# An RWKV scan in a two-layer network: substitution of two chunks at once, four product buffers, preparation in halves

## The chip, the core and the metric

The kernel is one program on one core of a Trainium2 chip. The metric is device time in microseconds from one launch to its end. Five engines work beside each other, each in the order of its own queue, and wait for one another by semaphores: TensorE (PE; its weight loads PEld), VectorE (DVE), ScalarE (ACT), GpSimd (POOL) and SyncE (SP), which issues the DMAs.

## The reference, cut to what matters

The network takes 256 context rows and 256 latent rows of 1,024 columns, in float32. Its first layer mixes them with RWKV-7 and Mamba side by side; attention, experts and a second block of two layers follow. The change lies in the RWKV part: per head (8 heads of 64 x 64) a state runs over 256 context rows and then over 256 latent rows, once forward and once backward.

```python
def step(S, inp):                       # per row: r, w, k, v, a, b
    sa = jnp.einsum('bhvk,bhk->bhv', S, a_t)
    S = S * w_t[:, :, None, :] + sa[..., None] * b_t[:, :, None, :] + v_t[..., None] * k_t[:, :, None, :]
    return S, jnp.einsum('bhvk,bhk->bhv', S, r_t)
...
logw = rw_w0 + tanh(lw) @ rw_w_up;  decay = exp(-exp(-softplus(-logw) - 0.5))
iclr = sigmoid(rw_a0 + la @ rw_a_up)
kk = k * rw_k_k / max(norm(k * rw_k_k), 1e-12)          # norm per head
k_dir = k * (1 + (iclr - 1) * rw_k_a);  a = -kk;  b = kk * iclr
bonus = (sum(r * k_dir_f * r_k0) + sum(r * k_dir_b * r_k1)) * v
```

## The kernel before, in words

Channels lie on partitions and rows on columns. `mixer_in` leaves the projections in `zrw` (12 blocks of 128 channels x 512 rows: k, r, v) and `lg` (low-rank inputs). The RWKV stage then runs in three parts.

*Preparation* (`rwkv_prep`, L646): for all 512 rows, in four blocks `j` of 128 channels and both directions `d`, low-rank products (L675, L682) with full 128-row weights, sigmoids, a running sum `cs` of the decay within each chunk (L679), `kd` (L685, L686), the scaled k (L689) and `b` (L691, on GpSimd). The three arrays `cs`, `b`, `kd` have their own memory, on the other side of the working space.

*Scan* (`rwkv`, L693): both directions at once, in eight steps of 64 rows. Forward takes the chunks 0 to 7, backward 3, 2, 1, 0, 7, 6, 5, 4. For step `n`:
- `products(n)`: scaled factors `ar` and `bkp` (L734 to L741, on DVE and GpSimd), their products on TensorE (L750), masked into `g` by DVE (L751), and the transposed `bkp` into `bt` (L758, L760). `bkp` has one buffer, `ar`, `g` and `bt` three.
- `base(n)`: inverts the 16 x 16 diagonal blocks of (1 - lower part of `g`) by forward substitution on DVE: cuts (L768 to L771), then 15 steps of a shuffle (L777), a product (L780) and a sum (L782), 8 heads x 16 columns wide and narrower at each step.
- `inverse(n)`: expands them into `st` (L788) and doubles the blocks twice, each time with a DVE transpose (L793), a mask on GpSimd (L796), products on TensorE (L800, L804), ACT in between and a sum (L805).
- `values(n)`: v transposed by products with the identity (L815), evicted by ACT.
- `through(n)`: the recurrence. State X times `ar` (L829) plus `g` times v (L832), evicted as `z`, times `st` (`up_`, L836), evicted, the state's update on TensorE (L843) and DVE (L848, L849), and the output (L854 to L861).

In program order the loop takes `through(n)`, `values(n+1)`, `inverse(n+1)`, `base(n+2)`, `products(n+3)`, then the bonus and `rwkv_out` of a half where it is complete, then `FILL` = 6 chunks of modulation (`ada_rest`, L396 to L405: 256 KB weight loads and products, 26 chunks in all, independent of the scan).

*Handover*: `layer0` halves the results into `cathi` and `catlo` (L947, L948) and starts the output projection (`mix_out`), whose weights come by SP (L329) and are split by ACT and DVE (L347, L348).

The order on each engine isn't written out by hand here: `TileContext(nc, schedule_with_timeline_sim=True)` lets a planner choose it with its own costs, in which an earlier place in the program gives precedence. A tile's buffer is given out again when its last reader is done.

Of the kernel before, what the change touches and what calls it, by code (L numbers as in the profile page):

```python
# [26 lines left out]
FILL = 6  # L27
# [66 lines left out]
def host_arrays(inp):  # L94
# [75 lines left out]
    lo = _Pack()  # L170
    for d in range(2):
        lo.add(f"w_up{d}", _rows_to(g["rw_w_up"][0, d], at=32 * d))
        lo.add(f"a_up{d}", _rows_to(g["rw_a_up"][0, d], at=64 + 32 * d))
    lo.add("g_up", _rows_to(g["rw_g_up"][0]))
    A["lora"] = lo.array()
# [14 lines left out]
    return A, pk.at, lo.at, {name: pack.at for name, pack in cst.items()}  # L190
# [75 lines left out]
class Net:  # L266
    def __init__(self, ctx, tc, ins, at, out):
        self.tc, self.nc, self.ins, self.out = tc, tc.nc, ins, out
        self.par_at, self.lora_at, self.cst_at = at
# [376 lines left out]
    def rwkv_prep(self, zrw, lg, arr, pool):  # L646
        nc = self.nc
        mm = nc.tensor.matmul
        lora = pool.tile([P, 2048], F32, name="lora", bufs=1)
        nc.sync.dma_start(lora, self.ins["lora"][:, :2048])  # L650
        o = {n: a for n, (a, _) in self.lora_at.items()}
        reset = pool.tile([P, T], F32, name="reset", bufs=1)
        nc.gpsimd.memset(reset, 1.0)
        nc.gpsimd.memset(reset[:, ::64], 0.0)
        tl = pool.tile([P, T], F32, name="tl", bufs=1)
# [5 lines left out]
        nc.sync.dma_start(lg[:, 0], self.ins["lora"][:, 2048:2560])  # L661
        ssp = self.bank(2, [8, T])
        for j in range(4):
            kq = pool.tile([P, T], F32, name="pq")
            nc.scalar.activation(kq, zrw[:, j], AF.Square, scale=self.p("k_k", j))
            mm(ssp, self.c("sel")[:, 8 * j:8 * j + 8], kq, start=j == 0, stop=j == 3)
        nrm = pool.tile([8, T], F32, name="pq")
        nc.scalar.activation(nrm, ssp, AF.Sqrt)
        nc.vector.tensor_scalar(nrm, nrm, 1e-12, None, op0=ALU.max)
        nc.vector.reciprocal(nrm, nrm)  # L670
        for j in range(4):
            ic = [pool.tile([P, T], F32, name=f"ic{d}") for d in range(2)]
            for d in range(2):
                wp = self.bank(0, [P, T])
                mm(wp, lora[:, o[f"w_up{d}"] + j * P:o[f"w_up{d}"] + (j + 1) * P], tl, start=True, stop=True)  # L675
                sg = pool.tile([P, T], F32, name="pq")
                nc.scalar.activation(sg, wp, AF.Sigmoid, bias=self.p(f"w0{d}", j))
# [3 lines left out]
                ap = self.bank(1, [P, T])  # L681
                mm(ap, lora[:, o[f"a_up{d}"] + j * P:o[f"a_up{d}"] + (j + 1) * P], tl, start=True, stop=True)  # L682
                nc.scalar.activation(ic[d], ap, AF.Sigmoid, bias=self.p(f"a0{d}", j))
                kd = arr["kd"][:, d, j]
                nc.vector.tensor_scalar(kd, ic[d], self.p("k_a", j), ka1[:, j:j + 1], op0=ALU.mult, op1=ALU.add)  # L685
                nc.vector.tensor_mul(kd, kd, zrw[:, j])  # L686
            rp = self.bank(3, [P, T])
            mm(rp, self.c("selt")[0:8, j * P:(j + 1) * P], nrm, start=True, stop=True)
            nc.vector.scalar_tensor_tensor(zrw[:, j], zrw[:, j], self.p("k_k", j), rp, op0=ALU.mult, op1=ALU.mult)  # L689
            for d in range(2):  # L690
                nc.gpsimd.tensor_mul(arr["b"][:, d, j], zrw[:, j], ic[d])  # L691

    def rwkv(self, zrw, arr, lg, y, pool, fill):  # L693
# [7 lines left out]
        first, second = (up, dn), (dn, up)  # L701
        bcast = lambda m, n: m[:, None, :].to_broadcast([m.shape[0], n, m.shape[1]])
# [10 lines left out]
        S16 = {}  # L713

# [6 lines left out]
        def products(n):  # L721
            ch, tok = tokens(n)

# [4 lines left out]
            ar = AR[n] = pool.tile([P, 2, 4, P], F32, name="ar", bufs=3)  # L728
            for d in range(2):
                a0, b0 = first[d], second[d]  # L730
                cs = arr["cs"][:, d, :, tok[d]]
# [6 lines left out]
                nc.vector.tensor_mul(bkp[up, d, :, 0, a0], arr["b"][up, d, :, tok[d]], ei[up, d])  # L738
                nc.gpsimd.tensor_mul(bkp[dn, d, :, 1, a0], arr["b"][dn, d, :, tok[d]], ei[dn, d])
                nc.gpsimd.tensor_mul(bkp[up, d, :, 0, b0], arr["kd"][up, d, :, tok[d]], ei[up, d])  # L740
                nc.gpsimd.tensor_mul(bkp[dn, d, :, 1, b0], arr["kd"][dn, d, :, tok[d]], ei[dn, d])  # L741
# [3 lines left out]
            g = G[n] = [pool.tile([P, 8, P], F32, name=f"g{d}", bufs=3) for d in range(2)]  # L745
            for d in range(2):
                for odd, r in ((0, up), (1, dn)):
# [5 lines left out]
            bt = BT[n] = pool.tile([P, 2, 4, P], F32, name="bt", bufs=3)  # L753
            tp = [self.bank(1, [P, 2, 4, 64]) for _ in range(2)]
            for d in range(2):
                for j in range(4):
                    for odd, r in ((0, up), (1, dn)):
                        tr(tp[odd][:, d, j], bkp[r, d, j, odd], ident[r, r])  # L758
            for odd, r in ((0, up), (1, dn)):
                ev(bt[:, :, :, r], tp[odd])  # L760

        def base(n):

            c32 = pool.tile([P, 8, 32], F32, name="c32", bufs=1)
            for q in range(4):
                rq = slice(32 * q, 32 * q + 32)
                at = 64 * (q // 2) + 32 * (q % 2)
                nc.vector.tensor_copy(c32[rq], G[n][q // 2][rq, :, at:at + 32])  # L768
            c16 = pool.tile([P, 8, 16], F32, name="c16", bufs=1)
            nc.vector.tensor_scalar(c16, c32[:, :, 0:16], self.c("half")[:, 0:1], None, op0=ALU.mult)  # L770
            nc.vector.scalar_tensor_tensor(c16, c32[:, :, 16:32], self.c("half")[:, 1:2], c16,  # L771
                                           op0=ALU.mult, op1=ALU.add)
            s = S16[n] = pool.tile([P, 8, 16], F32, name="s16")
            nc.gpsimd.tensor_copy(s, bcast(self.c("id16"), 8))
            for k in range(15):
                lb = pool.tile([P, 8, 16], F32, name="lb", bufs=3)
                nc.vector.stream_shuffle(lb[:, :, k + 1:], c16[:, :, k + 1:],  # L777
                                         [16 * (q // 16) + k for q in range(32)])
                m = pool.tile([P, 8, 16], F32, name="lm", bufs=2)
                nc.vector.tensor_mul(m[:, :, k + 1:], lb[:, :, k + 1:],  # L780
                                     s[:, :, k:k + 1].to_broadcast([P, 8, 15 - k]))
                nc.vector.tensor_add(s[:, :, k + 1:], s[:, :, k + 1:], m[:, :, k + 1:])  # L782

        def inverse(n):
# [3 lines left out]
            nc.vector.tensor_mul(st.rearrange("p h (g c) -> p h g c", g=4),  # L788
# [18 lines left out]
        def values(n):  # L807
# [3 lines left out]
            vr = pool.tile([P, 4, 64], F32, name="vr", bufs=1)  # L811
            nc.gpsimd.tensor_copy(vr, zrw[:, 8:12, tok[1]])
            for d, rows in ((1, up), (0, dn)):
                for j in range(4):
                    mm(vp[rows, j], vr[:, j] if d else zrw[:, 8 + j, tok[0]], ident, start=True, stop=True,  # L815
                       skip_group_check=True)
                ev(uv[rows, d], vp[rows].rearrange("p j (h v) -> p (j h) v", h=2))

        def through(n):
# [19 lines left out]
            if n < 7:  # L839
                for d in range(2):  # L840
# [23 lines left out]
        products(0)  # L864
        base(0)
        values(0)
        inverse(0)
        products(1)
        base(1)
        products(2)  # L870
        for n in range(8):
# [4 lines left out]
            if n < 6:  # L876
                base(n + 2)
            if n < 5:
                products(n + 3)
            if n in (3, 5):  # L880
                self.bonus(n // 4, zrw, arr)
# [10 lines left out]
    def bonus(self, half, zrw, arr):  # L892
# [3 lines left out]
        for j in range(4):  # L896
            e = arr["b"][:, 1, j, at]
            nc.vector.tensor_scalar(e, arr["kd"][:, 0, j, at], self.p("r_k0", j), None, op0=ALU.mult)
            nc.vector.scalar_tensor_tensor(e, arr["kd"][:, 1, j, at], self.p("r_k1", j), e,
# [50 lines left out]
    def layer0(self, run, late):  # L950
# [3 lines left out]
        with ExitStack() as mix:  # L954
# [15 lines left out]
            with ExitStack() as ph:  # L970
                self.stream(ph, RAWS, 512, 0, "right")
                arrp = pool(ph, "arr", side="right")
                arr = {k: arrp.tile([P, 2, 4, T], F32, name=k) for k in ("cs", "b", "kd")}
                with ExitStack() as c:
                    self.rwkv_prep(zrw, lg, arr, pool(c, "pw", 2))
                with ExitStack() as c:
                    rw = pool(c, "rw", 2)
                    self.rwkv(zrw, arr, lg, cat[:, 0:4], rw, self.ada_rest([(0, n) for n in range(8, 24)] + [(1, n) for n in range(EARLY)], rw, 0, 1))
# [1068 lines left out]
```

## Time and profile before

| | |
|---|---|
| median of 3 runs | 3051.7 us (3050.88 to 3053.53) |
| profiled execution | 3049.1 us, span 3047.3 us |
| TensorE busy | 2935.5 us, 96% of the span |
| DVE busy | 2113.2 us, 69% |
| ACT busy | 1592.5 us, 52% |
| GpSimd busy | 774.2 us, 25% |

Busy shares are means over stages with different limits; the stage of the change (some 230 to 570 us) is read by itself. A group of instructions gives its line, engine, operation, tiles out<-in, shapes and count, then the busy time of the group, the mean of one and the idle time of the engine just before them. A float32 matmul is recorded as two passes, a transpose as one. In a timeline `[3.41 <-POOL ...]` is idle time and what ended it.

### The profile page before, as it was taken

To read this page: it belongs to the slowest core of one execution; us is meant where nothing else is said; L and a number is where in the kernel's file an instruction comes from. 1 tells how busy PE (TensorE), PEld (TensorE's weight loads), DVE (VectorE), ACT (ScalarE), POOL (GpSimd) and SP (SyncE) were. 2 spreads that over 40 slices of the span, in tenths; PEclk is the share of its full clock that TensorE was granted. 3 is DMA by queue.
4 is the path that set the end of the run, shared out by engine and by line. 5 is a ranking of instruction groups with operands and counts; after the bars stand their busy time and mean duration, and the time that the engine had idled before them with its cause. 6 is when DMAs were issued, how large, how long until landed. Compare 5 with 4: busy or idle time off the path is not lost. (4 is left out here: it accounts for less than half of the span.)

```text
span 3047.3 us, 44960 instructions
## 1 busy us (share of the span) xinstructions
PE 2935.5 (96%) x17880; PEld 2453.4 (81%) x17880; DVE 2113.2 (69%) x2953; ACT 1592.5 (52%) x2007; POOL 774.2 (25%) x719
## 2 busy tenths in 40 slices
PE   7997899999999998999999999999999999999998
PEld 5884677887888777888888888878888888888887
DVE  5658987622223654998888898977697666669665
ACT  5644223432222555777777776755445545545553
POOL 0335442211022112000000000035264534434552
PEclk9998799999999999999999999999999999999999
DMA  6222234244423334999999999955533555553453
GB/s 229 70 66 70 84 111 148 104 166 146 137 75 114 110 97 154 346 359 331 363 345 337 357 350 362 340 176 186 197 132 120 192 175 199 170 195 107 150 176 128
DMA packets 132456, 584.75 MB, mean 192 GB/s; under 512 B 11792, under 2 KB 48912, under 8 KB 79760
## 3 DMA queue, kind: packets, MB, share of 16 engines
q1 hardware_dynamic: 126592, 575.35, 53.2%
q10 hardware_dynamic: 5648, 6.47, 0.9%
q8 instruction: 142, 2.33, 0.3%
q14 instruction: 74, 0.61, 0.1%
HBM read 580.73 MB, written 1.05 MB: 191 GB/s over the span
## 5 line engine op out<-in xcount | busy, mean ns | idle before, releaser
L348 DVE TENSOR_TENSOR wlo<-raw,whi 128x2048 fp32r<-128x2048 f32 (+2 forms) x497 | 1059.3, 2139 | 243.3 <-ACT whi L347 204.9
L347 ACT ACTIVATE whi<-raw 128x2048 fp32r<-128x2048 f32 (+2 forms) x500 | 886.5, 1784 | 418.8 <-PE bank L362 195.6
L372 PE MATMUL bank<-a,whi 128*128 128x512 f32 x1408 | 355.4, 395 | 5.1 <-DVE a L1693 5.1
L372 PEld LDWEIGHTS bank<-a,whi 128*128 128x128 f32 x1408 | 256.0, 190 | 51.7 <-DVE a L1693 5.4
L1361 PE MATMUL bank<-whi,xghi 128*128 128x512 f32 x704 | 282.3, 401 | 0.0
L1362 PE MATMUL bank<-whi,xglo 128*128 128x512 f32 x704 | 276.6, 393 | 0.0
L348 POOL TENSOR_TENSOR wlo<-raw,whi 128x2048 fp32r<-128x2048 f32 x3 | 13.9, 4646 | 790.2 <-ACT whi L347 790.2
L361 PE MATMUL bank<-cathi,whi 128*128 128x512 f32 (+1 forms) x608 | 212.6, 368 | 1.4 <-ACT x L1264 1.0
L362 PE MATMUL bank<-catlo,whi 128*128 128x512 f32 (+1 forms) x608 | 211.6, 364 | 1.5 <-DVE catlo L454 1.5
L375 PEld LDWEIGHTS bank<-a,wlo 128*128 128x128 f32 x1408 | 191.8, 190 | 13.6 <-DVE wlo L348 0.4
L375 PE MATMUL bank<-a,wlo 128*128 128x256 f32 x1408 | 196.5, 283 | 0.0
L1364 PE MATMUL bank<-wlo,xghi 128*128 128x512 f32 x704 | 192.2, 394 | 0.0
L1748 POOL TENSOR_TENSOR g<-gs,g 128x256 fp32r<-128x256 f32 x88 | 153.0, 1740 | 97.3 <-ACT g L1747 97.3
L372 PE MATMUL bank<-g,whi 128*128 128x512 f32 x704 | 171.2, 391 | 0.1
L1362 PEld LDWEIGHTS bank<-whi,xglo 128*128 128x128 f32 x704 | 132.4, 188 | 26.7
L1361 PEld LDWEIGHTS bank<-whi,xghi 128*128 128x128 f32 x704 | 132.2, 188 | 27.0
L1364 PEld LDWEIGHTS bank<-wlo,xghi 128*128 128x128 f32 x704 | 129.9, 188 | 29.6 <-DVE wlo L348 2.1
L372 PEld LDWEIGHTS bank<-g,whi 128*128 128x128 f32 x704 | 128.4, 188 | 24.4 <-POOL g L1748 0.3
L1613 PE MATMUL bank<-whi,gthi 128*128 128x512 f32 x352 | 139.7, 397 | 0.0
L361 PEld LDWEIGHTS bank<-cathi,whi 128*128 128x128 f32 x608 | 114.7, 190 | 29.3 <-issue 8.3
L1613 PE MATMUL bank<-whi,gtlo 128*128 128x512 f32 x352 | 138.1, 392 | 0.0
L364 PE MATMUL bank<-cathi,wlo 128*128 128x512 f32 (+1 forms) x608 | 136.4, 362 | 0.0
(530 smaller groups left out, 5883.1 us busy)
## 6 DMA issues: line engine op xcount, KB each, us to landing
raw<-in_moei_dram SPq DMA_DIRECT2D x155, 1024.0 KB, 5.7
raw<-in_sfi_dram SPq DMA_DIRECT2D x88, 1024.0 KB, 4.8
raw<-in_moeo_dram SPq DMA_DIRECT2D x77, 1024.0 KB, 5.2
raw<-in_sfo_dram SPq DMA_DIRECT2D x64, 704.0 KB, 4.1
raw<-in_ada_dram SPq DMA_DIRECT2D x104, 256.0 KB, 3.6
raw<-in_smi_dram SPq DMA_DIRECT2D x24, 1024.0 KB, 4.8
raw<-in_ffi_dram SPq DMA_DIRECT2D x22, 1024.0 KB, 4.9
x<-in_moei_dram SPq DMA_DIRECT2D x21, 1024.0 KB, 5.8
```

Source lines behind the costliest of these rows:

```text
L347: self.nc.scalar.activation(like(hi, w)[:, c], w[:, c], AF.Copy)
L348: (eng or self.nc.vector).tensor_sub(like(lo, w)[:, c], w[:, c], like(hi, w)[:, c].bitcast(F32))
L361: mm(ps, l, a[0][:, ak[j]], start=start and j == 0, stop=False, skip_group_check=True)
L362: mm(ps, l, a[1][:, ak[j]], start=False, stop=False, skip_group_check=True)
L364: mm(ps, w[1][:, wk[j], f0:f0 + fn], a[0][:, ak[j]], start=False, stop=stop and j == n - 1, skip_group_check=True)
L372: mm(ps.rearrange("p i s -> p (i s)"), w[0][:, wk[j], f0:f0 + P], a[:, ak[j]].rearrange("p i s -> p (i s)"), start=start and j == 0, stop= ...
L375: mm(ps[:, 0], w[1][:, wk[j], f0:f0 + P], a[:, ak[j], 0], start=False, stop=stop and j == n - 1, skip_group_check=True)
L1361: mm(ps, a[0][:, at + k, rows], w[0][:, k, cols], start=start and n == 0, stop=False, skip_group_check=True)
L1362: mm(ps, a[1][:, at + k, rows], w[0][:, k, cols], start=False, stop=False, skip_group_check=True)
L1364: mm(ps, a[0][:, at + k, rows], w[1][:, k, cols], start=False, stop=stop and n == len(ks) - 1, skip_group_check=True)
L1613: mm(y[f], g.bitcast(F32) if self.whole else g, w[q][:, i, 512 * f:512 * f + 512], start=n == q == i == p == 0, stop=n == 10 and i == 1 an ...
L1748: nc.gpsimd.tensor_sub(lo, s, hi.bitcast(F32))
```

## The change

- The low-rank weights are packed in 32-row groups (w0, w1, a0, a1 below each other), so one load of 512 columns instead of 2,048, and each product reads 32 rows, into banks 1 and 2 instead of 0 and 1.
- `rwkv_prep` works on 256 rows (`half`), and the arrays `cs`, `b`, `kd` hold one half, in the scan's pool, with one buffer. The first half is prepared ahead of the scan, the second in step 0, behind `bonus(0)`. The scan's pool opens ahead of the preparation.
- `base` takes two chunks: cuts by 16 ACT copies with a scale and one GpSimd sum, then the same 15 steps over 16 x 16 columns, the product in place.
- L788 moves to GpSimd. `values` gathers both directions on GpSimd and does 4 transposes. The state's product with `wc` covers 128 partitions at once.
- `ar`, `g` and `bt` have four buffers; `products(0)` to `products(3)` come ahead of step 0. `FILL` is 4.

```diff
-            for d in range(2):
-                wp = self.bank(0, [P, T])
-                mm(wp, lora[:, o[f"w_up{d}"] + j * P:o[f"w_up{d}"] + (j + 1) * P], tl, start=True, stop=True)
...
+            acc = [self.bank(k, [P, S]) for k in (1, 1, 2, 2)]
+            for q in range(4):
+                r = slice(32 * q, 32 * q + 32)
+                mm(acc[q], lora[r, j * P:(j + 1) * P], tl[r, at], start=True, stop=True)
...
+        def prep(half):
+            arr.update({k: pool.tile([P, 2, 4, S], F32, name=k, bufs=1) for k in ("cs", "b", "kd")})
+            return self.rwkv_prep(half, zrw, dict(arr), made, pool)
...
-        def base(n):
+        def base(ns):
+            m = 8 * len(ns)
+            cut = [pool.tile([P, 16, 16], F32, name=name, bufs=1) for name in ("c16", "lb")]
+            for i, n in enumerate(ns):
+                for q in range(4):
+                    rq = slice(32 * q, 32 * q + 32)
+                    at = 64 * (q // 2) + 32 * (q % 2)
+                    for k in range(2):
+                        nc.scalar.activation(cut[k][rq, 8 * i:8 * i + 8], G[n][q // 2][rq, :, at + 16 * k:at + 16 * k + 16],
+                                             AF.Copy, scale=self.c("half")[rq, k:k + 1])
+            c16 = cut[0][:, :m]
+            nc.gpsimd.tensor_add(c16, c16, cut[1][:, :m])
+            s = pool.tile([P, 16, 16], F32, name="s16")
+            nc.gpsimd.tensor_copy(s[:, :m], bcast(self.c("id16"), m))
             for k in range(15):
-                lb = pool.tile([P, 8, 16], F32, name="lb", bufs=3)
+                lb = pool.tile([P, 16, 16], F32, name="lb", bufs=1)
...
-            nc.vector.tensor_mul(st.rearrange("p h (g c) -> p h g c", g=4),
+            nc.gpsimd.tensor_mul(st.rearrange("p h (g c) -> p h g c", g=4),
...
+            for d, rows in ((1, up), (0, dn)):
+                nc.gpsimd.tensor_copy(vr[:, :, rows], zrw[:, 8:12, tok[d]])
+            for j in range(4):
+                tr(vp[:, j], vr[:, j], ident)
...
-                        nc.vector.tensor_mul(xn[r, :, r], xn[r, :, r], wc[r].to_broadcast([64, 4, 64]))
+                    nc.vector.tensor_mul(xn, xn, wc.to_broadcast([P, 4, P]))
...
+        for _ in prep(0):
+            pass
+        for n in range(2):
+            products(n)
+        base((0, 1))
         values(0)
         inverse(0)
-        products(1)
-        base(1)
-        products(2)
+        for n in range(2, 4):
+            products(n)
         for n in range(8):
             through(n)
             if n < 7:
                 values(n + 1)
                 inverse(n + 1)
...
+            if n == 0:
+                base((2, 3))
+                self.bonus(0, zrw, arr)
+                for _ in prep(1):
+                    pass
+            if n == 1:
+                products(4)
+                products(5)
+            if n == 2:
+                base((4, 5))
+                products(6)
+            if n == 3:
+                products(7)
+                base((6, 7))
+                self.bonus(1, zrw, arr)
```

## Rows read from the trace of the kernel before

**Rows 1.** Busy time by engine in four stretches: PE, PEld, DVE, ACT, POOL; then clock, DMA share, GB/s.
```profile
237.80:268.30 30.50, 20.60 (x55) 6.14 (x53) 29.36 (x30) 15.20 (x23) 13.32 (x6) 0.88 0.07 22
268.30:342.90 74.60, 57.47 (x552) 42.84 (x554) 62.01 (x234) 16.76 (x40) 44.83 (x62) 0.73 0.40 135
342.90:540.40 197.50, 182.71 (x2482) 149.97 (x2479) 165.42 (x546) 64.09 (x126) 69.22 (x87) 0.97 0.31 105
590.00:700.00 110.00, 110.00 (x695) 91.36 (x694) 40.78 (x63) 35.80 (x53) 17.20 (x7) 1.00 0.38 135
```

**Rows 2.** Timeline of PE, `up_` of steps 0 and 7: start, us, engine, line.
```profile
342.90 1.16 PE L836 MATMUL bank<-z,st 64*64 64x64 f32 x32
...
540.35 1.15 PE L836 MATMUL bank<-z,st 64*64 64x64 f32 x32 [0.42 <-ACT z L703]
```

**Rows 3.** DVE by line, 229 to 568 us: count, busy us, mean ns, idle before.
```profile
L780 DVE TENSOR_TENSOR lm<-lb,s 128x120 f32<-128x120 f32 (+14 forms) x120 | 39.7, 332 | 0.5
L782 DVE TENSOR_TENSOR s<-s,lm 128x120 f32<-128x120 f32 (+14 forms) x120 | 37.3, 311 | 3.1
L777 DVE STREAM_SHUFFLE lb<-c 128x120 f32<-128x120 f32 (+14 forms) x120 | 26.9, 234 | 0.0
...
L849 DVE TENSOR_TENSOR X<-X,wc 64x256 f32<-64x256 f32 x28 | 15.0, 536 | 0.6
L768 DVE COPY c<-g 32x256 f32<-32x256 f32 x32 | 14.2, 445 | 0.6
...
L788 DVE TENSOR_TENSOR st<-s,cst_scan 128x512 f32<-128x512 f32 x8 | 6.0, 754 | 0.2
...
L771 DVE SCALAR_TENSOR_TENSOR c<-c,cst_scan,c 128x128 f32<-128x128 f32 x8 | 4.9, 617 | 0.1
```

**Rows 4.** Timeline of DVE, shuffles of `base(7)`: start, us; then widths.
```profile
488.32 0.26 DVE L777 STREAM_SHUFFLE lb<-c 128x80 f32<-128x80 f32 x1
...
488.94 0.26 DVE L777 STREAM_SHUFFLE lb<-c 128x72 f32<-128x72 f32 x1
...
494.21 0.19 DVE L777 STREAM_SHUFFLE lb<-c 128x24 f32<-128x24 f32 x1
...
494.68 0.18 DVE L777 STREAM_SHUFFLE lb<-c 128x16 f32<-128x16 f32 x1
```

**Rows 5.** Timeline of DVE, lead-in: `bkp`, last `g` of chunks 0 and 1, `st`.
```profile
273.71 0.52 DVE L738 TENSOR_TENSOR bkp<-b,ei 64x256 f32<-64x256 f32 x1 [3.41 <-POOL bkp L709]
...
287.37 0.68 DVE L751 TENSOR_TENSOR g<-bank,cst_scan 128x512 f32<-128x512 f32 x1
...
299.78 0.69 DVE L751 TENSOR_TENSOR g<-bank,cst_scan 128x512 f32<-128x512 f32 x1 [0.69 <-PE bank L750]
...
321.05 1.21 DVE L788 TENSOR_TENSOR st<-s,cst_scan 128x512 f32<-128x512 f32 x1
```

**Rows 6.** TensorE by line, 229 to 568 us: count, busy us, mean ns.
```profile
L396 PE MATMUL bank<-raw,c 128*32 128x256 f32 x416 | 42.7, 452 | 19.4 <-DVE mod L405 13.4 <-ACT pq L677 3.9 <-DMA raw<-in_ada_dram 1.2
...
L815 PE MATMUL bank<-cst_all,vr 128*64 128x128 f32 x64 | 9.5, 294 | 2.3 <-POOL vr L812 2.3
...
L675 PE MATMUL bank<-tl,lora 128*128 128x512 f32 x16 | 8.5, 625 | 2.6 <-ACT pq L677 2.5
```

**Rows 7.** GpSimd by line, 229 to 568 us: busy us, mean ns, idle before.
```profile
L796 POOL TENSOR_TENSOR lmask<-g,cst_scan 64x512 f32<-64x512 f32 x32 | 41.1, 1285 | 24.8 <-PE bank L800 22.5 <-DVE g L751 1.0
L691 POOL TENSOR_TENSOR b<-zrw,ic 128x512 f32<-128x512 f32 x8 | 15.8, 2014 | 29.8 <-DVE zrw L689 27.3 <-ACT ew L732 2.5
```

**Rows 8.** Timeline of ACT and SP at the handover to the output projection.
```profile
523.42 1.15 ACT L947 ACTIVATE cathi<-x 128x512 fp32r<-128x512 f32 x2 [3.97 <-PE bank L903]
...
523.46 27.26 SPq L329 DMA_DIRECT2D raw<-in_mixout_dram  x3
```

**Rows 9.** Waits of the scan, 342.9 to 540.4 us: total us, times, longest us.
```profile
POOL bkp L740 <- PE bank L758: 7.3, 3, 4.3
```

**Rows 10.** One line of DVE: durations in ns, minimum, median, maximum.
```profile
L780 DVE TENSOR_TENSOR lm<-lb,s x120: 134/223/1296, 293.6 to 498.2; 128x120 f32<-128x120 f32 x8, 128x112 f32<-128x112 f32 x8, 128x104 f32<-128x104 f32 x8, 128x96 f32<-128x96 f32 x8
```

More of the change, by code (lines that the diff above doesn't have):

```diff
@@ L26 @@
 FIRST = 4
-FILL = 6
+FILL = 4
 RAWS = 4
@@ L189, in host_arrays @@
         A[f"cst_{name}"] = pack.array()
[L190 removed]
+    return A, pk.at, {name: pack.at for name, pack in cst.items()}
 def _consts():
@@ L642, in mamba, with rwkv_first @@
             yield
-    def rwkv_prep(self, zrw, lg, arr, pool):
+    def rwkv_first(self, lg, pool):
         nc = self.nc
[L648 to L652, printed above, removed]
+        lora = pool.tile([P, 512], F32, name="lora", bufs=1)
+        nc.sync.dma_start(lora, self.ins["lora"][:, :512])
+        reset = pool.tile([P, S], F32, name="reset", bufs=1)
         nc.gpsimd.memset(reset, 1.0)
         nc.gpsimd.memset(reset[:, ::64], 0.0)
-        tl = pool.tile([P, T], F32, name="tl", bufs=1)
+        tl = self.sq
         nc.scalar.activation(tl[0:64], lg[0:64, 0], AF.Tanh)
@@ L660, in rwkv_prep @@
         nc.vector.tensor_scalar(ka1, self.p("k_a"), -1.0, 1.0, op0=ALU.mult, op1=ALU.add)
-        nc.sync.dma_start(lg[:, 0], self.ins["lora"][:, 2048:2560])
-        ssp = self.bank(2, [8, T])
+        nc.sync.dma_start(lg[:, 0], self.ins["lora"][:, 512:1024])
+        return lora, reset, tl, ka1
+    def rwkv_prep(self, half, zrw, arr, made, pool):
+        nc = self.nc
+        mm = nc.tensor.matmul
+        lora, reset, tl, ka1 = made
+        at = slice(S * half, S * half + S)
+        ssp = self.bank(2, [8, S])
         for j in range(4):
-            kq = pool.tile([P, T], F32, name="pq")
-            nc.scalar.activation(kq, zrw[:, j], AF.Square, scale=self.p("k_k", j))
+            kq = pool.tile([P, S], F32, name="pq")
+            nc.scalar.activation(kq, zrw[:, j, at], AF.Square, scale=self.p("k_k", j))
             mm(ssp, self.c("sel")[:, 8 * j:8 * j + 8], kq, start=j == 0, stop=j == 3)
-        nrm = pool.tile([8, T], F32, name="pq")
+        nrm = pool.tile([8, S], F32, name="nrm", bufs=1)
         nc.scalar.activation(nrm, ssp, AF.Sqrt)
@@ L701, in rwkv @@
         first, second = (up, dn), (dn, up)
+        both = ((0, up), (1, dn))
         bcast = lambda m, n: m[:, None, :].to_broadcast([m.shape[0], n, m.shape[1]])
@@ L713, in rwkv @@
         S16 = {}
+        made = self.rwkv_first(lg, pool)
+        arr = {}
+        def prep(half):
+            arr.update({k: pool.tile([P, 2, 4, S], F32, name=k, bufs=1) for k in ("cs", "b", "kd")})
+            return self.rwkv_prep(half, zrw, dict(arr), made, pool)
         def tokens(n):
@@ L722, in products @@
             ch, tok = tokens(n)
+            c0, c1 = (k % 4 for k in ch)
+            own = [slice(64 * c0, 64 * c0 + 64), slice(64 * c1 + 63, 64 * c1 - 1 if c1 else None, -1)]
             ew = pool.tile([P, 2, 4, 65], F32, name="ew", bufs=1)
@@ L737, in products @@
                                      ew[:, d, :, now if d == 0 else slice(64, 0, -1)])
[L738 to L741, printed above, removed]
+                nc.vector.tensor_mul(bkp[up, d, :, 0, a0], arr["b"][up, d, :, own[d]], ei[up, d])
+                nc.gpsimd.tensor_mul(bkp[dn, d, :, 1, a0], arr["b"][dn, d, :, own[d]], ei[dn, d])
+                nc.gpsimd.tensor_mul(bkp[up, d, :, 0, b0], arr["kd"][up, d, :, own[d]], ei[up, d])
+                nc.gpsimd.tensor_mul(bkp[dn, d, :, 1, b0], arr["kd"][dn, d, :, own[d]], ei[dn, d])
             wc = WC[n] = pool.tile([P, 2, 4], F32, name="wc", bufs=4)
             nc.gpsimd.tensor_copy(wc, ew[:, :, :, 64])
-            g = G[n] = [pool.tile([P, 8, P], F32, name=f"g{d}", bufs=3) for d in range(2)]
+            g = G[n] = [pool.tile([P, 8, P], F32, name=f"g{d}", bufs=4) for d in range(2)]
+            bt = BT[n] = pool.tile([P, 2, 4, P], F32, name="bt", bufs=4)
             for d in range(2):
-                for odd, r in ((0, up), (1, dn)):
+                for odd, r in both:
                     gp = self.bank(1, [P, 4, P])
@@ L756, in products @@
                 for j in range(4):
-                    for odd, r in ((0, up), (1, dn)):
+                    for odd, r in both:
                         tr(tp[odd][:, d, j], bkp[r, d, j, odd], ident[r, r])
-            for odd, r in ((0, up), (1, dn)):
+            for odd, r in both:
                 ev(bt[:, :, :, r], tp[odd])
-        def base(n):
[L764 to L774, printed above, removed]
+        def base(ns):
[12 more added lines that the diff above has]
+            nc.gpsimd.tensor_copy(s[:, :m], bcast(self.c("id16"), m))
@@ L971, in layer0 @@
                 self.stream(ph, RAWS, 512, 0, "right")
[L972 to L975, printed above, removed]
                 with ExitStack() as c:
                     rw = pool(c, "rw", 2)
-                    self.rwkv(zrw, arr, lg, cat[:, 0:4], rw, self.ada_rest([(0, n) for n in range(8, 24)] + [(1, n) for n in range(EARLY)], rw, 0, 1))
+                    self.rwkv(zrw, lg, cat[:, 0:4], rw, self.ada_rest([(0, n) for n in range(8, 24)] + [(1, n) for n in range(EARLY)], rw, 0, 1))
             cp = pool(late, "cp", side="right")
```

69 lines of the change are left out of this document (28 added, 41 removed).

## The prediction

> **What bounds the kernel now.** All of the change lies in the RWKV stage of the first layer, so I read by stage. First the busy time of each engine in four stretches [rows 1]: preparation of the scan (237.8 to 268.3), lead-in up to the first `up_` product (268.3 to 342.9), the eight scan steps up to the last `up_` (342.9 to 540.4), and, for comparison, a later projection (590 to 700). The reader is to see that no two have the same limit. The preparation is bound by DVE (29.36 of 30.5). The lead-in is DVE too (62.0 of 74.6), with TensorE at a granted clock of 0.73 of full speed, so between 1.2 and 2.4 GHz on average. In the scan DVE is busy for 165.4 of 197.5 but TensorE for 182.7, so 92.5%: it has 14.8 us of idle time to give back. In the later stretch TensorE is busy for all of 110.0, so time won in the stage isn't lost again behind it.
>
> The timeline of TensorE then gives the marks [rows 2]: `up_` of step 0 begins at 342.90, of step 7 at 540.35, so 197.45 us for seven steps, 28.2 each. That last one waited for ACT's `z`, not for the substitution's `st`. By lines DVE's largest work in the stage is the substitution in `base` [rows 3].
>
> The sum is made against the profiled execution: 3049.1 us, of which the span is 3047.3. The median of the runs is 3051.7, 2.6 more, and I add those 2.6 at the end.
>
> **The change, part by part.**
>
> *Substitution in pairs.* One step is a shuffle, a product and a sum. Undisturbed steps lie 0.62 us apart (488.32 to 488.94, some 91 columns per instruction) and 0.47 apart (494.21 to 494.68, some 35 columns) [rows 4]. That is 0.0027 us per column and a fixed 0.38 us. A chunk has 15 steps and 8 x 120 = 960 columns: 5.7 + 2.6 = 8.3 us. A pair has 15 steps and 1,920 columns: 5.7 + 5.2 = 10.9. Under way it costs more: the three lines sum to 39.7 + 37.3 + 26.9 = 103.9 us [rows 3], and since successive instructions overlap (three of some 0.26 each in a pitch of 0.62 [rows 4]) that is 83 us of DVE, 10.3 per chunk, 1.24 times the undisturbed. With that factor a pair costs 13.5, four pairs 54. Gone: 83 - 54 = 29. The cuts out of `g` (L768, L771, 14.2 + 4.9 = 19.1) go to ACT and GpSimd; so 48 in all. ACT gets 64 copies of 32x128; at most as long as its 128x512 copies (1.15 for two [rows 8]), 37 us, in an engine busy for 64.1 of 197.5 and 16.8 of 74.6 [rows 1]. Only the last eight, behind the second chunk's `g`, stand on the path.
>
> *Other DVE work.* The expansion of `st` (6.0, L788) goes to GpSimd. The product with `wc` becomes 14 of 128x512, priced as L788's mean of 0.75, 10.5 instead of 15.0 [rows 3]. Splitting the preparation adds some 30 instructions at a fixed 0.13 (estimate: a third of a step's 0.38): +4. DVE in all: -48 - 6 - 4.5 + 4 = -55.
>
> *TensorE.* `values` had 128 passes, 9.5 us for the 64 of one of its two groups [rows 6], so some 19; now 32 transposes, at the same 0.148 each 4.7. So -14, of which 12 in the scan. The low-rank products had two groups of 16 passes like L675's 8.5, 17 us; now 64 passes of 256 columns and 32 rows. If the four row groups run beside each other as the four column groups of the modulation do (42.7/416 = 0.103 each [rows 6]) that is 7; one after the other, at half of L675's 0.53, 17. I take 7, the nearer in kind (four groups of 32): -10; the other end is no gain.
>
> *Lead-in.* Half of the preparation stays ahead: 29.4/2 + 2 = 16.7 instead of 30.5, so -13.8. The clearing of `bkp`, for which DVE waited 3.41 us at 273.71 [rows 5], stood behind the whole preparation since its pool opened then; it now opens ahead: -3.4. Then the chain. The first chunk's `g` ends at 288.05, the second's at 300.47, 12.4 later, with pieces of `base` among them [rows 5]; without these I take 10. Last cuts, and the sum of the halves on GpSimd: 3 (at most 8 x 0.58). Paired substitution 14, and 2 for what DVE does in between. `inverse` and the head of step 0: 342.90 - 321.05 = 21.9 now, 21.3 with the expansion on GpSimd and a product or two of other work less. Sum 50.3 instead of 342.90 - 288.05 = 54.9: -4.6. Lead-in in all **-22** (-14 if the chain gains nothing and the clearing stays, -30 if it runs at the undisturbed pace).
>
> *Scan.* TensorE: 182.7, less 12 (`values`), less 3.5 (a fourth `products` goes ahead: 48 of 2,482 passes), plus 5 (second preparation: (20.6 - 10)/2), plus 5 (two modulation chunks that the shorter lead-in no longer holds; `FILL` 4 only spreads them) = 177. At its present share of 92.5% that is 191.5 us, at 97% 182.5; so -6 to -15, and I take **-10**. DVE: 165.4 less two thirds of 48, less 4 (L788), less 4 (`wc`), less 5 (one `products`), plus 16 (second preparation), plus 3 (bonus 0, which lay in the lead-in) = 139 of 187. DVE is no longer first; the DVE time saved here is mostly TensorE's to give. The second preparation has a wait of its own: its arrays have one buffer, so it waits for `products(3)` and `bonus(0)`, and behind its first scan in DVE's queue stand the state updates. Its result is due at step 4: 15 + 32 (two `products`, as 268.3 to 300.5) + 14 + 21 = 82 us behind step 0, against four steps at 26. It is in time, with 22 us to spare.
>
> *Handover.* Output weights and `cathi` took the place of the arrays of the preparation: both started at 523.4, when bonus(1) let go of them [rows 8], 17 us ahead of the last `up_`. Now the arrays lie in the scan's own pool, with four buffers for `ar`, `g`, `bt` beside them, and the place comes free with the last scan tiles. I take **+3** (0 to +8: a load and a split, of which the output half of step 7 hides some). Smaller low-rank loads, `tl` in an old buffer, the host's packing: nothing, SP and DMA wait for nobody here (share 0.07 and 0.40 [rows 1]).
>
> Sum: -22 - 10 + 3 = -29; 3049.1 - 29 + 2.6 = **3022**. Own range -12 to -45: 3007 to 3040.
>
> **Rivals.**
>
> *A, DVE is the bound after all and all of its 55 us come off:* 3049.1 - 55 + 2.6 = 2997. For it: before 342.9 it is so, and TensorE's 92.5% is partly filled with passes that fill gaps. Against: only 14.8 us of TensorE idle in the scan. The Trainium skill (Perfetto Trace Analysis, Identifying the Most-Contended Engine) holds matmul busy time for a bad measure and wants the share of weight loads. By it TensorE has a quarter of the scan free and A is the case. The trace: weight loads 150.0 of 197.5, 76%, but also only 83% (91.4 of 110.0) where TensorE is never idle [rows 1], so 76% is nine tenths of what is reached; I leave A one chance in five.
>
> DVE's products in `base` have a median of 223 ns and a maximum of 1,296 [rows 10], while GpSimd's own take 1,285 (L796) to 2,014 [rows 7]. The Trainium skill (SBUF — State Buffer, Who interferes with whom) says why: a DVE instruction with two SBUF inputs and a GpSimd one that reads shut each other out for a whole instruction. By it the eight expansions and four sums moved to GpSimd take up to 12 x 1.3 = 16 us of DVE back, and A would give 3013. The trace agrees that such stops occur, not that each does.
>
> *B, the second preparation beside the scan costs the scan:* it holds all of banks 1 and 2 in each of four blocks, which the scan's state products, `inverse` and `products` use as well; TensorE's queue stops behind them until ACT has done four sigmoids. Four blocks at some 4 us (four ACT evictions of 0.58 and two small products): +16, so 3038. For it: queues are in order. Against: the 22 us in hand.
>
> *N, nothing left:* B, the full handover (+5) and low-rank products one after the other (+5): -3, 3049.
>
> *S, slower: the substitution's expansion in GpSimd's queue.* `inverse` now begins on GpSimd, behind `products` pieces that wait for TensorE up to 4.3 us each [rows 9], and takes 1.3 to 2.0 instead of 0.75. If `st` then comes last at each `up_`, eight times (4.3 + 1.25) = 44: -29 + 44 = +15, 3067. It decides from 35/8 = 4.4 us per chunk. Against: at step 7 `z` was last [rows 2], and with four chunks ready ahead `inverse` may run early.
>
> **Chances.** Forecast 0.48, A 0.20, B 0.15: faster by over 0.2% (6.1 us, about what a measurement of this kernel tells from none) 0.83. N: 0.07 within. S: 0.10. The range goes from below A, 2988, to N, 3048; it leaves out S and A's lower end.
>
> **What would show it.** Right: first `up_` near 320, last near 508; 60 shuffles instead of 120 with a pitch of some 0.7; in the scan TensorE above 92% and DVE near 75%; output weights loaded later against the last `up_` than now. Wrong: a scan above 195 us with TensorE waiting for evictions in banks 1 or 2 (B), `up_` waiting for DVE's `st` (S), or a scan below 175 us with DVE above 80% (A).

## The result, and the profile after

The changed kernel takes 3082.5 us (median of 4 runs, 3075.23 to 3086.92) against 3052.55 for the kernel before in the same rounds: ratio 1.0098 [1.0085, 1.0112], so 30 us slower where 29 us faster was forecast. The profiled execution after has a span of 3083.0 us, 35.7 more than before; 33.8 of them have come up by the last `cathi`, 2.2 ahead of the stage (its last input projection product ends at 235.47 instead of 233.25).

Windows of the kernel after, stages as in [rows 1] and in its columns; the last row is the stretch of the second preparation:

```profile
237.80:268.30 30.50, 24.23 (x140) 12.00 (x134) 16.88 (x36) 16.85 (x35) 9.01 (x15) 0.68 0.49 163
268.30:351.90 83.60, 70.06 (x622) 48.66 (x622) 53.73 (x151) 28.54 (x68) 40.79 (x54) 0.71 0.44 147
351.90:570.20 218.30, 195.85 (x2279) 156.41 (x2279) 139.29 (x340) 90.52 (x175) 87.58 (x108) 0.83 0.18 61
...
380.00:430.00 50.00, 48.41 (x310) 32.64 (x310) 27.87 (x51) 27.26 (x50) 20.83 (x28) 0.62 0.17 56
```

DVE did shrink as forecast (139 us in the scan). But the scan is longer by 20.9 us, and TensorE, busy for 48.41 of 50 us in the second preparation, does 310 matmuls there at a granted clock of 0.62: near 1.2 instead of 2.4 GHz for most of it.

TensorE's timeline after: `up_` (L857) of steps 0, 1, 2 and 7, as in [rows 2], with low-rank products (L682) and state products of step 1 (L864) between:

```profile
351.89 1.15 PE L857 MATMUL bank<-z,st 64*64 64x64 f32 x32
...
379.00 0.56 PE L857 MATMUL bank<-z,st 64*64 64x64 f32 x10
...
395.34 1.22 PE L682 MATMUL bank<-sqsum,lora 32*128 32x256 f32 x2
...
398.65 2.08 PE L864 MATMUL bank<-uv,bt 128*128 128x128 f32 x8
...
401.86 1.22 PE L682 MATMUL bank<-sqsum,lora 32*128 32x256 f32 x2 [0.49 <-ACT ic L689]
403.01 2.08 PE L864 MATMUL bank<-uv,bt 128*128 128x128 f32 x8
...
437.91 0.91 PE L857 MATMUL bank<-z,st 64*64 64x64 f32 x22
...
570.16 0.80 PE L857 MATMUL bank<-z,st 64*64 64x64 f32 x20 [0.26 <-DVE st L826]
```

From these marks and those of before (342.9, 364.0, 391.8, 540.4): lead-in +9.0 us, step 0 to 1 +6.0 (27.1 against 21.1), step 1 to 2 **+31.1** (58.9 against 27.8), steps 2 to 7 -16.3 (132.3 against 148.6), last `up_` to last `cathi` +4.0 (31.2 against 27.2). One step shows as much loss as the whole. The lead-in is the least certain of these: the kernels whose code is the same up to step 0 (after, e1, e7, e8, e10 and e11 below) begin their first `up_` at 345.4 to 354.0 in their profiled executions, so +9.0 stands for +2.5 to +11.1.

DVE (238 to 606 us) and TensorE (238 to 602) by line, answering to [rows 3] and [rows 6]:

```profile
L801 DVE TENSOR_TENSOR s<-s,lb 128x240 f32<-128x240 f32 (+14 forms) x60 | 24.2, 403 | 1.4
...
L799 DVE TENSOR_TENSOR lb<-lb,s 128x240 f32<-128x240 f32 (+14 forms) x60 | 21.4, 356 | 1.5
L797 DVE STREAM_SHUFFLE lb<-c 128x240 f32<-128x240 f32 (+14 forms) x60 | 19.2, 319 | 0.1
...
L870 DVE TENSOR_TENSOR X<-X,wc 128x512 f32<-128x512 f32 x14 | 10.6, 755 | 0.2
L691 DVE TENSOR_SCALAR kd<-ic,par,ka 128x256 f32<-128x256 f32 x16 | 7.2, 449 | 21.3 <-ACT ic L689 21.3
```

```profile
L682 PE MATMUL bank<-sqsum,lora 32*128 32x256 f32 x64 | 23.5, 592 | 3.8 <-ACT pq L685 2.4 <-ACT ic L689 1.3
```

The substitution's three lines went from 103.9 to 64.8 us. The low-rank products, forecast at 7 us, are busy for 23.5.

The time that a substitution takes fell by less than its busy time. VectorE's timeline after, one step at 32 columns and the start of the next:

```profile
358.14 0.22 DVE L797 STREAM_SHUFFLE lb<-c 128x32 f32<-128x32 f32 x1
358.39 0.19 DVE L799 TENSOR_TENSOR lb<-lb,s 128x32 f32<-128x32 f32 x1
358.62 0.19 DVE L801 TENSOR_TENSOR s<-s,lb 128x32 f32<-128x32 f32 x1
...
358.85 0.22 DVE L797 STREAM_SHUFFLE lb<-c 128x16 f32<-128x16 f32 x1
```

The three now follow one another, 0.71 us from shuffle to shuffle; before, shuffles ran ahead of the sums, and a step of some 35 columns took 0.47 [rows 4]. At 224 columns it is 1.33 (500.16 to 501.49). By these two a pair takes some 15 us undisturbed (an estimate: 15 steps at a fixed 0.61 and 1,920 columns at 0.0032), against 16.6 for two chunks before and the forecast's 10.9 for a pair. `lb`, which the shuffle writes, had three buffers before and has one now, with the product in place. That this is the reason isn't shown: no run changes it alone, and e2, e4 and all runs made from the kernel after have it.

### The profile page after: what moved, and what is told of

Same layout as the page of the kernel before. It is cut to its first block, busy times and chain, and to the rows that moved or that the text cites. A ratio compares the mean times of both kernels' runs of the same rounds, so it can differ in the third digit from the quotient of the medians.

```text
span 3083.0 us, 44714 instructions
## 1 busy us (share of the span) xinstructions
PE 2961.3 (96%) x17832; PEld 2470.3 (80%) x17832; DVE 2070.3 (67%) x2673; ACT 1633.6 (53%) x2100; POOL 788.2 (26%) x743
## 5 line engine op out<-in xcount | busy, mean ns | idle before, releaser
L1391 PEld LDWEIGHTS bank<-whi,xghi 128*128 128x128 f32 x704 | 132.2, 188 | 27.1 <-ACT xgf L1566 0.3
```

Of the source, the lines that this page charges most:

```text
L1391: mm(ps, a[0][:, at + k, rows], w[0][:, k, cols], start=start and n == 0, stop=False, skip_group_check=True)
```

## The experiments

Theory T: the second preparation beside the scan makes the loss. Rivals: the pairs, the small moves, table loads on ScalarE, the fill, the place in program order. All medians stand against the kernel before in the same rounds.

| run | edit | us against before | ratio, 95% interval |
|---|---|---|---|
| after | | +30.0 | 1.0098 [1.0085, 1.0112] |
| e1 | after, no second preparation | -5.5 | 0.9981 [0.9972, 0.9991] |
| e2 | before + pairs | +10.8 | 1.0030 [1.0018, 1.0041] |
| e3 | before + small moves | +14.7 | 1.0048 [1.0034, 1.0063] |
| e4 | before + both | +19.6 | 1.0060 [1.0043, 1.0077] |
| e5 | e3, v in `z`'s buffer | +1.1 | 1.0011 [1.0001, 1.0020] |
| e6 | after, v in `z`'s buffer | +24.1 | 1.0079 [1.0062, 1.0096] |
| e7 | e1, pair (4, 5) a step earlier | -8.3 | 0.9976 [0.9967, 0.9986] |
| e8 | after, preparation 2 in its own bank | +27.5 | 1.0102 [1.0084, 1.0120] |
| e9 | after, 128-row low-rank products | +18.9 | 1.0064 [1.0048, 1.0081] |
| e10 | after, no sigmoids in preparation 2 | +29.0 | 1.0101 [1.0084, 1.0118] |
| e11 | after, fill between its blocks | +30.5 | 1.0106 [1.0090, 1.0123] |
| e12 | e5, `st` on VectorE | +0.6 | 1.0008 [0.9998, 1.0018] |
| e13 | after, one chunk at a time | +32.4 | 1.0102 [1.0085, 1.0119] |
| e14 | e13 + e9 + e6 | +15.9 | 1.0055 [1.0038, 1.0072] |
| e15 | e14, `st` on VectorE | +14.6 | 1.0047 [1.0030, 1.0064] |
| e16 | e15 + e8 | +37.7 | 1.0123 [1.0106, 1.0140] |
| e17 | e16, products(4), (5) a step later | +38.7 | 1.0125 [1.0108, 1.0142] |
| e18 | before, `FILL` 4 | +2.8 | 1.0011 [1.0001, 1.0020] |

**e1, the second preparation left out.**

```diff
-                for _ in prep(1):
-                    pass
```

> The changed kernel without the second preparation (rows 256 to 511 use the arrays of the first half: the output is not the reference's). Theory T: the second preparation beside the scan makes the loss (step 1 to 2 takes 58.9 us instead of 27.8), so about 30 us go: 3048 to 3058 us. Rival C (the second preparation only fills gaps, the scan is slow by the pairing, the GpSimd expansion or the clock): under 8 us go, 3075 to 3083 us.

Measured: 35.5 us go between +30.0 and -5.5, more than the 30 expected. T holds, and step 1 to 2 takes 21.2 us. But what is left of the change, with half of the preparation not done at all, gains only 5.5.

**e2, pairs alone; e3, small moves alone; e4, both.**

```diff
-            base(0) ... base(n + 2)
+            base((0, 1)) ... if n in (0, 2, 4): base((n + 2, n + 3))     # e2, three buffers
...
+            nc.gpsimd.tensor_mul(st...)  # e3, with the transposes of values and the merged product with wc
```

> The kernel before with nothing but the substitution of two chunks at once (cuts on ScalarE, three buffers, preparation of all rows ahead). T: DVE loses some 29 us of pairs and 19 us of cuts, the lead-in waits for products(1) but does one substitution less: 8 to 22 us faster than before, 3030 to 3044 us. Rival P (two chunks at once bind inverse(n) to products that come later, and 16 copies wait in ScalarE's queue): 3055 to 3070 us.

> The kernel before with nothing but the expansion st on GpSimd, the values by 4 transposes and the product with wc over 128 partitions. T: 14 us of TensorE in the scan and 8 us of DVE are off, 1 us per step waits in GpSimd's queue: 3038 to 3052 us. Rival S (the expansion waits behind the masks in GpSimd's queue): 3055 to 3067 us.

> The kernel before with the pairs of e2_pair and the three moves of e3_small; preparation of all rows ahead, three buffers, FILL 6. T (only the preparation in halves is at fault): the sum of the two, 3020 to 3040 us, faster than both kernels. Rival C (the scan itself is slow with these parts): 3055 to 3080 us.

All three slower, so T alone doesn't explain the change. In e2 the pair (2, 3) waits for products(3), and inverse(2) with it. VectorE's timeline of e2: the last shuffle of the pair, the expansions, the transposition that opens inverse(2):

```profile
395.22 0.22 DVE L779 STREAM_SHUFFLE lb<-c 128x16 f32<-128x16 f32 x1
...
396.59 1.29 DVE L791 TENSOR_TENSOR st<-s,cst_scan 128x512 f32<-128x512 f32 x2
397.80 0.70 DVE L796 STREAM_TRANSPOSE tt<-st 128x512 f32<-128x512 f32 x1
```

Before, the same transposition ran at 357.55: `up_` of step 2 comes at 411.1 instead of 391.8. With three buffers a pair is late for its first chunk.

**e5, e6, e12: the gathered v.** In e3's timelines of TensorE, then ScalarE, inverse(2)'s products (L800) end at 374.6, but `hh` is evicted at 383.32:

```profile
374.01 0.63 PE L800 MATMUL bank<-tt,lmask 64*64 64x64 f32 x8
...
379.22 1.16 PE L843 MATMUL bank<-uv,bt 128*128 128x128 f32 x8
380.30 1.15 PE L854 MATMUL bank<-uv,g 128*64 128x64 f32 x18
381.39 0.66 PE L815 MATMUL bank<-cst_all,hh 128*128 128x128 f32 x4
```

```profile
383.32 0.60 ACT L703 ACTIVATE hh<-bank 128x512 f32<-128x512 f32 x1
```

`values` had put its v into `hh`'s only buffer, and its transposes (L815) stand behind the state products in TensorE's queue.

```diff
-            vr = pool.tile([P, 4, P], F32, name="hh", bufs=1)
+            vr = pool.tile([P, 4, P], F32, name="z", bufs=1)      # e5 in e3, e6 in after; e12: st on VectorE too
```

> e3_small with one name changed: the gathered v of values(n+1) lies in the buffer of z instead of that of hh. In e3_small hh of an inverse is evicted only when the transposes of values are done, and these stand behind the state's products in TensorE's queue (products ready at 374.6 us, hh evicted at 383.3). Theory H (this shared buffer is the loss of the small moves): 8 to 18 us less than e3_small, 3045 to 3057 us. Rival S (st behind the masks in GpSimd's queue is the loss): no change, 3060 to 3068 us.

> The changed kernel with the same one name changed. H: the steps 2 to 7, which wait for inverse, come 5 to 15 us earlier, 3067 to 3078 us. Rival T2 (only the second preparation paces these steps): within 3 us of the changed kernel, 3079 to 3086 us.

> e5_small_z with the expansion st on DVE again: the kernel before with nothing but the values by 4 transposes (gathered in the buffer of z) and the product with wc in one. If st on GpSimd costs (1.28 us against 0.75 in the chain of inverse): 2 to 8 us less than e5_small_z, 3046 to 3052 us. Rival (st is off the path, the chain of inverse(n) sets the pace whatever TensorE has less to do): 3051 to 3055 us.

H holds in e5: 13.6 us back, and `hh` follows its products at once. In the changed kernel it is 6 us by the medians, with intervals that overlap. With the buffer mended the small moves cost next to nothing (+1.1) and win nothing; `st` on GpSimd can't be told from `st` on VectorE.

**e7, the pair (4, 5) earlier.**

```diff
+                base((4, 5))      # n == 1, behind products(5)
             if n == 2:
-                base((4, 5))
```

> e1_skip2 (no second preparation) with the substitution of chunks 4 and 5 one step earlier in the program, in step 1 behind products(5). In e1_skip2 inverse(4) starts at 450.6 us, when that substitution is done, 27 us behind the end of inverse(3). Theory P (a pair is late for its first chunk): 8 to 20 us less, 3025 to 3037 us. Rival (the substitution is paced by DVE's other work or by TensorE and not by its place): 3040 to 3048 us.

No difference: the pair's 45 instructions run from 409.6 to 449.8 us, in e1 from 407.7 to 447.6. What releases them is products(5), and VectorE does `rwkv_out`, products(6) and the bonus between them.

**e8, banks; e10, tables; e11, fill.**

```diff
+        bank = lambda k, s: self.bank(0, s, 1) if half else self.bank(k, s)   # e8, one after the other
...
-                nc.scalar.activation(sg, acc[d], AF.Sigmoid, bias=self.p(f"w0{d}", j))
+                nc.scalar.activation(sg, acc[d], AF.Exp, scale=1e-3)       # e10, second half; ic too
...
-                    pass
+                    next(fill, None)                                       # e11
```

> The changed kernel with all PSUM tiles of the second preparation in one bank that the scan does not use (one product after the other), instead of banks 1 and 2. Theory B (the banks are given out in program order, so inverse(2) and the state's products of step 1 wait until the second preparation has let them go): 15 to 33 us less than the changed kernel, 3050 to 3068 us. Rival L (ScalarE's eight table loads and TensorE's in-order queue make the loss): 3075 us or more.

> The changed kernel with Exp of a small argument in place of the sigmoids of the second preparation (so the gates of rows 256 to 511 are not computed; same instructions on ScalarE, no change of table between them and the exponentials of products). Theory A (table loads: 8 x 1.283 us on ScalarE, in the chain of the second preparation): 8 to 14 us less, 3068 to 3075 us. Rival K: the table loads lie beside TensorE's slow products, under 4 us, 3078 to 3084 us.

> The changed kernel with a chunk of the modulation after each of the five blocks of the second preparation. Theory F (with FILL 4 behind the second preparation TensorE lacks other work there, and its clock falls): 5 to 15 us less, 3067 to 3078 us. Rival (the planner orders TensorE by readiness, place changes nothing): 3079 to 3088 us.

e8 did free step 1 to 2 (32.8 us instead of 58.9) and the time stayed: steps 2 to 4 took 86.4 instead of 69.8. e10 took six of eight table loads out of the stretch from 365 to 425 us and e11 moved the fill, both without a difference.

**e9, 128-row low-rank products.**

```diff
-                mm(acc[q], lora[r, j * P:(j + 1) * P], tl[r, at], start=True, stop=True)
+                mm(acc[q], lora[:, j * P:(j + 1) * P], wide[:, q], start=True, stop=True)   # wide: zero outside r
```

> The changed kernel with its low-rank products over 128 rows again: lora whole, tl copied by GpSimd into four copies that are zero outside their 32 rows (in y, not yet written there). The result is the same. Theory K (with 32-row products TensorE falls to 1.2 GHz though it is busy: clock 0.50 at 250 to 270 us and 0.50 to 0.62 at 390 to 420 us, busy 92 to 100%, where the kernel before kept 1.00 with 72 to 92% busy in 128-row products): the clock of both preparations rises above 0.8 and 10 to 25 us go, 3057 to 3073 us. Rival L (the clock falls because TensorE waits for ScalarE and the single buffers): clock and time as in the changed kernel, 3078 to 3090 us.

Measured: 11 us less, intervals apart. Windows of e9, columns as above, then its low-rank products (ns: minimum, median, maximum):

```profile
380.00:430.00 50.00, 44.46 (x511) 32.31 (x511) 34.43 (x59) 31.51 (x61) 30.67 (x40) 1.00 0.26 86
```

```profile
L684 PE MATMUL bank<-x,lora x64: 379/379/796, 244.0 to 404.4; 128*128 128x256 f32 x64
```

The same stretch holds 511 matmuls at clock 1.00 instead of 310 at 0.62. Theory K holds for the second preparation: its last scan ends at 397.1 instead of 403.3, step 1 to 2 takes 46.2 us. In the lead-in the clock rose too (0.96 instead of 0.50 at 250 to 260, 0.73 instead of 0.50 at 250 to 270), but the first `up_` stayed where it was, at 351.8.

**e13, one chunk at a time in the changed kernel; e14 and e15, edits together.**

```diff
-        base((0, 1))
+        base((0,))      # then base((n + 2,)) in step n
```

> The changed kernel with the substitution of one chunk at a time (all else as changed). Theory P (a pair delays its first chunk): inverse(0) waits for one chunk, up_(0) comes before 340 instead of at 351.9 us, and inverse(4) no longer waits 27 us behind inverse(3): 8 to 22 us less, 3060 to 3074 us. Rival D (VectorE is the bound: 55 us more of it): 3085 to 3110 us.

> The changed kernel with three edits undone or mended together: one chunk at a time, 128-row low-rank products, the gathered v in the buffer of z. If the three causes add up: 3082 less 13, 6 and 8 to 22: 3041 to 3055 us. If they hide each other (the step that waits longest sets the pace): 3056 to 3068 us.

> e14_mix with the expansion st on VectorE as in the kernel before. GpSimd's 1.28 us against 0.75 stands in the chain of each inverse: 2 to 6 us less than e14_mix. Rival: within 2 us of it.

TensorE's timeline of e13: the first `up_` comes 9.5 us earlier than in the changed kernel (3.0 to 11.6 earlier than in the six with the same lead-in), where P had said before 340:

```profile
342.37 1.97 PE L857 MATMUL bank<-z,st 64*64 64x64 f32 x32 [0.80 <-DVE st L826]
```

The end didn't move: steps 1 to 2 still took 62.0 us, the scan 225.3 instead of 218.3, and the last `up_` is at 567.6. What the lead-in wins, the scan mostly gives back. Both P and D failed. e14 is 14 us under the changed kernel, not clearly under e9: the edits hide each other, as the second expectation had it, and do not reach the kernel before. e15 is 1.4 us under e14, with intervals that overlap.

**e16 and e17: banks with fast products; e18, `FILL`.**

```diff
+                products(4)      # e17: n == 2 instead of n == 1; products(5) too
```

> e15_mix_dve with the second preparation's PSUM tiles in one bank of their own, one product after the other. Theory B (inverse(2) and the state's products of step 1 wait for banks 1 and 2; with TensorE at 2.4 GHz nothing else holds them): 8 to 16 us less than e15_mix_dve, at or under the kernel before, 3028 to 3048 us. Rival (one bank in turn makes the second preparation, and products(4) behind it, late by as much): within 4 us of e15_mix_dve.

> e16_mix_bank with products(4) and products(5) emitted in step 2, behind through(2), instead of step 1, and products(6) in step 3. Theory B2 (bank 1 is given out in program order: the state's products of step 2 wait for products(4) and (5) and so for the second preparation): they start within 8 us of up_(2), step 2 to 3 takes 25 to 35 us instead of 52, and 10 to 22 us go: 3066 to 3078 us. Rival W (the work of the second preparation itself paces the scan, wherever it waits): under 5 us go, 3083 to 3090 us.

> The kernel before with FILL 4 instead of 6, nothing else. If the filling chunks only use TensorE's gaps: within 3 us of the kernel before, 3048 to 3054 us. Rival F (fewer chunks per step leave TensorE idle early in the scan and crowd its end): 5 to 15 us slower, 3056 to 3066 us.

TensorE's timeline of e16, then of e17: `up_` of step 2 (L869) and the state products that follow it (L876).

```profile
396.35 1.97 PE L869 MATMUL bank<-z,st 64*64 64x64 f32 x32
...
425.48 0.71 PE L788 MATMUL bank<-cst_all,bkp 64*128 64x64 f32 x8
426.12 2.05 PE L876 MATMUL bank<-uv,bt 128*128 128x128 f32 x16
```

```profile
396.65 1.97 PE L869 MATMUL bank<-z,st 64*64 64x64 f32 x32
398.55 1.93 PE L393 MATMUL bank<-raw,c 128*32 128x256 f32 x16
401.68 2.07 PE L876 MATMUL bank<-uv,bt 128*128 128x128 f32 x8 [1.20 <-ACT uv L723]
```

B2's mechanism is there: the state products come 29.8 us after `up_`, behind products(4) and (5); in e17 they come 5.0 us after it. Its price is not: the time is the same, W holds. `up_` of step 4 comes at 478.8, 474.9, 482.4 and 478.9 us in e14 to e17, wherever the waiting is put. What it waits for last differs: in e14 and e17 inverse(4)'s `st` (ready at 478.79 and 478.46), in e16 the recurrence's `z` (483.05, its `st` at 472.33). That e16 is 23 us slower than e15, where both of its expectations had less or the same, has another cause in sight: the preparation sits in the modulation's bank, the modulation's last products end at 579.6 us, behind the scan, and the output weights begin at 571.1 instead of 534.2. This was not tested by itself. `FILL` 4 alone costs 2.8 us, by its interval 0.3 to 6.

No run beats the kernel before but e1 and e7, which leave work out.

## Why the prediction was wrong

*The step that failed: "82 us behind step 0 ... It is in time, with 22 us to spare."* In the trace after, `up_` of step 4 comes 155.8 us behind step 0. The marks, on VectorE the end of bonus(0), the last scan of the preparation, the last `g` of products(5) and the last shuffle of the pair (4, 5), then on TensorE `up_` of step 4:

```profile
368.74 0.42 DVE L938 TENSOR_TENSOR zrw<-zrw,bank 128x256 f32<-128x256 f32 x1
...
402.63 0.68 DVE L687 TENSOR_TENSOR_SCAN cs<-reset,pq 128x256 f32<-128x256 f32 x1
...
443.55 0.69 DVE L770 TENSOR_TENSOR g<-bank,cst_scan 128x512 f32<-128x512 f32 x1 [0.83 <-PE bank L769]
...
488.47 0.22 DVE L797 STREAM_SHUFFLE lb<-c 128x16 f32<-128x16 f32 x1
```

```profile
507.68 1.97 PE L857 MATMUL bank<-z,st 64*64 64x64 f32 x32 [0.83 <-DVE st L826]
```

Part by part, forecast first: the start was taken as 0, but bonus(0) lets go of the single buffers 17.3 us in; the preparation 15, measured 34.1 (to 403.3); two `products` 32, 40.9 (to 444.2); the pair 14, 44.5 (to 488.7); `inverse` to `up_` 21, 19.0. Every part but the last was priced at the pace it has when nothing else is in its queue. The pair missed most, and little of that is the second preparation's doing: while it ran VectorE was busy for 40.91 of 44.5 us, with state updates, products(6), `rwkv_out` and the next bonus between its steps, and in e1 the pair took 39.9. The other side of the comparison was wrong as well, the other way: four steps at 26 make 104, but step 4 came 116.2 us behind step 0 before the change, and 116.7 in e1. Against that the chain is 39 us late.

*B was the right rival, mis-sized and half right in its mechanism.* Priced at 16 us, it cost 35.5 (after against e1). Its banks do stop `inverse` and the state products (e8, e16), but freeing them moves the wait to the next step. What the runs give back is 11 us for the 32-row products (e9). That the chain from bonus(0) over the preparation to inverse(4) sets the rest fits the kernel after, e14 and e17, where `up_` of step 4 waits for inverse(4) last (in e14 and e17 20 us later than before); it does not fit e16, and no run takes the chain apart. Of what e14 keeps, 13.0 us are there at its last `up_` (553.3 against 540.4) and 3.3 more at the last `cathi`.

*Low-rank products, -10.* This took four row groups as running beside each other; the other end, 17 us, was nearer. The 64 passes are busy for 23.5 us, and over 128 rows (e9) for 21.0. The shortest pass of 32 rows is 374 ns, the shortest of 128 rows 379 (e9). The Trainium skill (TensorEngine Tiling (Array Packing), Theoretical Speedup) gives up to four times for a contraction of at most 32. In the trace the first eight passes ran beside each other, in 0.71 us at 244.31; a four and two sixes took 1.06, 1.23 and 1.23 us, and nearly all the rest came in twos or singly.

*Lead-in, -22, measured +9.* Two terms failed. One stood at nothing: "Smaller low-rank loads ...: nothing, SP and DMA wait for nobody here". SP's timeline before and after, then TensorE's weight loads after:

```profile
195.15 0.37 SPq L650 DMA_DIRECT2D lora<-in_lora_dram  x1
```

```profile
239.25 0.42 SPq L647 DMA_DIRECT2D lora<-in_lora_dram  x1
```

```profile
244.31 0.31 PEld L682 LDWEIGHTS bank<-sqsum,lora 32*128 32x128 f32 x8 [0.52 <-DMA lora<-in_lora_dram]
```

The low-rank weights are now issued behind eight modulation loads in SP's queue (203.29 to 239.20) and land 5.0 us later, and the first low-rank product waits for them. The half preparation does take less, 24.9 us instead of 33.4 from that product to its last scaled k, but it starts at 244.31 instead of 234.98: the two cancel, and the first chunk's last `g` comes 4.3 us earlier (283.8 against 288.05), not 17.2. In e8 the load went out at 225.2 and the first product came at 237.4; no run moves the load alone.

The other term is the chain from the first chunk's last `g` to `up_`, 68.1 us (283.8 to 351.9) where 50.3 were forecast: 12.9 to the second chunk's last `g` (10), 7.1 for cuts and sum (3), 26.5 for the pair's shuffles (14; 303.7 to 330.2), 21.7 for the rest (23.3). That the pair is the main part agrees with e2 (first `up_` at 350.0 with the pair alone) and e13 (342.4 without it).

*Scan, -10.* The DVE sum was right to the microsecond, in part by luck: its largest term, the substitution, is busy for 64.8 us where 54 were forecast. And it mattered little: 36.5 us more of DVE in the scan (e13, 175.8) made the scan 7.0 us longer, and the transposes (e12, priced at -14 with `values`) moved nothing. "14.8 us of idle time to give back" took TensorE's 92.5% for a bound, against which e12 speaks; a pace set by the chain `products`, `base`, `inverse`, `up_`, with chunks of modulation in the gaps, fits the runs. The Trainium skill (Perfetto Trace Analysis, Identifying the Most-Contended Engine), by which busy matmul time is a bad measure, spoke against this step, and the trace agrees: busy 97% at 380 to 430 us, weight loads 65%. Only A, which I drew from it, was wrong too: DVE's share of the scan fell from 84% to 64% without a gain. Where the pair (4, 5) runs it is 92% all the same, so a mean over the scan doesn't show where an engine binds.

*S* did not come: e12 against e5, e15 against e14. Its sign did, `up_` waits for `st` at steps 4 and 7; but at step 4 GpSimd begins the expansion at 489.85, 0.1 us behind the pair's last sum, so its queue is not the cause there. *Handover*, +3: 4.0.

## What to carry to other kernels

A step that is moved beside a serial chain has to be priced along its whole path to its consumer, from the moment its buffers come free, with every queue at the pace it has in that stretch; busy sums of engines say nothing of it. Look first which event the next step waits for: work taken off an engine that only fills gaps is worth nothing. A load that came early can come last when its place in a queue moves, and a busy sum can fall while the elapsed time hardly does, when instructions that overlapped no longer do. And a buffer borrowed under a name that another chain uses is a wait (e5: 13.6 us from one word).

## What the runs showed of the hardware

TensorE at 1.2 GHz while busy: with 32-row products among its work the granted clock stood at 0.62 over 380 to 430 us with matmuls for 48.4 of 50 us; with 128-row products it was 1.00 with 44.5 of 50 (e9). Other runs agree over the same stretch: 0.60 to 0.63 with 32-row products in it (e6, e10, e11, e13), 0.83 to 0.93 with 128-row products (e14 to e17). The Trainium skill's page on ScalarE (ScalarE: Activation LUTs, What ACT_TABLE_LOAD costs) gives 1,283 ns for a table load, and that is what the trace has; six of them fewer, 7.7 us, did not change the time (e10).
